# A block product by seven: sums left to accumulating matmuls in a PSUM bank that is read in between

## The chip, the cores and the metric

The kernel runs on one core of a Trainium2 chip. The metric is the time of one execution in microseconds of the device, lower is better. Three runs of the kernel before took 3091.07 to 3096.7 us, with a median of 3095.03 us.

## The reference, cut to what matters

Three transformer layers on one sequence of S = 1024 tokens and D = 1024 features, in fp32. The change lies in the last part alone, the feed-forward network of the third layer:

```python
h  = rmsnorm(x, g_ffn) * (1 + scale2) + shift2                 # [1024, 1024]
up = causal_dwconv(h @ w_up, conv_w, conv_b)                   # w_up [1024, 5632], three taps a column
gate, val = split(up, 2)
x  = x + (1 + gate2) * ((silu(gate) * val) @ w_down)           # w_down [2816, 1024]
out = rmsnorm(x, g_final)
```

## The kernel before

Activations lie transposed: features on the 128 partitions, tokens along a row, in two halves of 512. Each fp32 operand is split into two parts (a rounded one, `hi`, and the rest, `lo`), and a product of operands takes three matmuls a chunk of 128 features (`mm3`): hi by hi, hi by lo, lo by hi. A split costs a cast on ACT (`operand`, L443) and a subtraction (`lo`, L169) on DVE or POOL.

The feed-forward network multiplies by the seven products of Strassen's algorithm in Winograd's form. `strassen` takes two blocks of 128 rows of weights (a pair) and both halves of tokens and of the contraction, and forms products P1 to P7, 12 matmuls of 128x512 each, so 84 for a pair. From them come four quarters of the result: c11 and c12 (tile `u`), c21 and c22 (tile `v`):

```
c11 = P1 + P2          U2 = P1 + P6         U3 = U2 + P7
c12 = U2 + P5 + P3     c22 = U3 + P5        c21 = U3 + P4
```

Before, each product has a PSUM bank of its own. P5 and P7 take the two halves (two banks) of a tile `s` of 1024 columns, of which there are two buffers; the others take tiles `m` of one bank, of which there are four. P1 and P5 are copied to SBUF by ACT (L493, L503). DVE adds c11 (L496), U2 (L505), U3 (L507), and the last terms of c12 (L509) and c21 (L510), each from one operand in PSUM and one in SBUF; POOL adds P5 to U2 and to U3 (L506, L508), all in SBUF.

There are 22 pairs for `w_up`, one block of the gate and one of the value each. A pair is followed by its two convolutions (`conv`: one ACT instruction, L1525, then two on DVE, L1527, for each of the two), the silu (ACT, L1542) and the product of gate and value (POOL, L1543). Then come twice four pairs for `w_down` (16 of the 22 chunks of the contraction; results go to DRAM as `y`), and the last six chunks by plain products (`down`), with the norm and the output.

`start_pairs` begins a group of pairs: for the first three pairs P1 and P2, which need the first token half alone; then the operands of the other products (`turn_ops`, 20 splits); then the rest of these three pairs. These are the early pairs: three for `w_up`, and three for each half of `w_down`, nine in all. The other 21 pairs run P1 to P7 in one go.

Weights' operands lie in tiles `wh`, of which there are eight, and for a cast into one of them ACT waits until PE has used it. A list scheduler sets the order on each engine, from the order of the program's text as priority and its own estimate of times. On the chip each engine works its queue strictly in order and waits for others by semaphores. Such a wait goes by tile: an instruction that writes one half of `s` also waits for earlier readers of its other half.

Of the kernel before, what the change touches and what calls it, by code (L numbers as in the profile page):

```python
# [18 lines left out]
S = 1024  # L19
# [25 lines left out]
def alternate(a, b):  # L45
    """steps of a and of b together"""
    for _ in a:
        next(b, None)
        yield
    yield from b  # L50
# [7 lines left out]
def ahead(tc, gen, offset):  # L58
    """steps of gen, scheduled before work that was emitted up to offset instructions earlier"""
    if not offset:  # L60
        yield from gen
        return
    while True:
        with tc.high_priority(offset):
            x = next(gen, drain)
        if x is drain:
            return
        yield x


def some(g, n):
    """n steps of g"""
    for _ in range(n):
        if next(g, drain) is drain:
            return
        yield


def merge(main, fill, lead=0):
    """emit one step of fill after each step of main"""  # L80
# [7 lines left out]
def pace(main, total, early, fill, n):  # L88
    """steps of early at once, then n steps of fill spread over main, whose steps give their weight"""
# [11 lines left out]
class Net:  # L101
# [18 lines left out]
    def load(self, tag, shape, dt=F32):  # L120
        """a tile to be loaded, but not long before its phase"""
# [10 lines left out]
    def t(self, tag, shape, dt=F32):  # L132
        """a tile of 4 KB a partition, seen in the shape"""
# [14 lines left out]
    def c(self, shape, name, dt=F32):  # L148
        """a constant, or columns that stay"""
# [8 lines left out]
    def small(self, cols, tag):  # L158
        """columns for a short time: the next of a few in turn"""
# [11 lines left out]
    def wblock(self, src, k, m, lo_eng=None):  # L171
        """src: DRAM [k*128, m]; returns [(hi, lo)] per contraction chunk, each [128, m]"""
        return self.wload([src], k, m, lo_eng)

    def wload(self, srcs, k, m, lo_eng=None):
        """blocks of columns side by side"""
# [10 lines left out]
    def mm3(self, out, ws, rs, start=True, stop=True):  # L187
        """out += sum_k ws[k]^T rs[k]; ws, rs: (hi, lo)"""
        n, last = 0, 3 * len(ws) - 1
        for (wh, wl), (rh, rl) in zip(ws, rs):  # L190
            for l, r in ((wh, rh), (wh, rl), (wl, rh)):
                self.nc.tensor.matmul(out, l, r, start=start and n == 0, stop=stop and n == last)  # L192
                n += 1

# [20 lines left out]
    def columns(self, tile_name, width, names):  # L215
        """vectors as columns [128, j]"""
# [23 lines left out]
    def mask_tile(self, name, op, pattern, mult):  # L240
        """0 where the condition holds, else -BIG"""
# [39 lines left out]
    def sigmoid(self, sg, z, src):  # L281
        """sg <- sigmoid(z); src: where |z| is read from (z or its PSUM source)"""
# [15 lines left out]
    def modulation(self, cs, w, bcol, names, acc_tag="t2", w_tag="wr", shared=()):  # L298
        """columns [128, 8] of each 1024 outputs of cs @ w + b; chunks in shared: on ScalarE and GpSimd"""
# [27 lines left out]
    def sum_cols(self, acc, out):  # L327
        """out [128, 8] <- sums over the partitions of acc"""
# [7 lines left out]
    def modulation_first(self, cs, w, bcol, g, nme, acc_tag, w_tag):  # L336
        """as modulation, half of the products on TensorE"""
# [24 lines left out]
    def scale_col(self, g, scale, name):  # L362
        """g * (1 + scale)"""
# [14 lines left out]
    def stat_sum(self, acc):  # L378
        """sum over partitions, on every partition (PSUM)"""
# [10 lines left out]
    def rsqrt_mean(self, out, sums, dim):  # L390
        """(sums / dim + eps)^-1/2"""
# [5 lines left out]
    def stat_end(self, acc, dim):  # L397
        """acc -> (sum over partitions / dim + eps)^-1/2 on every partition, in place"""
        return self.rsqrt_mean(acc, self.stat_sum(acc), dim)

    def new_xt(self, tags):
        """x^T of a token half: 8 chunks [128, 512] in len(tags) tiles"""
# [37 lines left out]
    def operand(self, x, tag="h4", eng=None):  # L440
        """x [128, 512], split"""
# [5 lines left out]
    def rows(self, w, c0, m=128):  # L447
        """loads columns c0.. of w as the rows of a block, by halves of the contraction"""
# [8 lines left out]
    def weights(self, load, early):  # L457
        """operands of two blocks of rows by the number of the product, the first two products' first"""
# [20 lines left out]
    def strassen(self, load, ops, box, tag, early=False):  # L479
        """two blocks of rows times h, [128, 1024] each; early: the products of the first token half, alone,  # L480
        in steps"""
# [4 lines left out]
        def product(ps, i):  # L486
            wv = ws[i].rearrange("p l (k m) -> p l k m", k=4)
            self.mm3(ps, [(wv[:, 0, k], wv[:, 1, k]) for k in range(4)], [(t[:, 0], t[:, 1]) for t in ops[i]])
# [3 lines left out]
        c11, p1 = u[:, 0:512], u[:, 512:]  # L492
        nc.scalar.copy(p1, product(self.pm(), 1))  # L493
        if early:
            yield
        nc.vector.tensor_add(c11, product(self.pm(), 2), p1)  # L496
        if early:
            yield
        next(wg)
        v, t = self.t(tag, [128, S]), self.t("t2", [128, 2, 512])  # L500
        c12, c21, c22, p5, u2 = p1, v[:, 0:512], v[:, 512:], t[:, 0], t[:, 1]
        ps = self.pS()
        nc.scalar.copy(p5, product(ps[:, 0:512], 5))  # L503
        p7 = product(ps[:, 512:], 7)
        nc.vector.tensor_add(u2, product(self.pm(), 6), p1)  # L505
        nc.gpsimd.tensor_add(c12, p5, u2)  # L506
        nc.vector.tensor_add(u2, p7, u2)  # L507
        nc.gpsimd.tensor_add(c22, p5, u2)  # L508
        nc.vector.tensor_add(c12, product(self.pm(), 3), c12)  # L509
        nc.vector.tensor_add(c21, product(self.pm(), 4), u2)  # L510
        box += [u, v]

    def next_h(self, proj, xbox, acc, acol, shift):
        """ends the projection; h of the next part (fp32, in the place of x), and the operands of its first
        token half"""
# [16 lines left out]
    def turn_ops(self, ops, b11, b12, b21, b22):  # L532
        """operands of a chunk of each half of the contraction, but the first two products'; in place"""
# [11 lines left out]
    def start_pairs(self, pair, n, chunk, ops):  # L545
        """the first pairs of blocks: what needs the first token half, the other operands, the rest"""
# [13 lines left out]
    def load_x(self):  # L560
        """tokens of x"""
# [1129 lines left out]
```

## Time and profile before

| what | value |
|---|---|
| time, median of 3 runs | 3095.03 us (3091.07 to 3096.7) |
| span of the profiled execution | 3102.5 us |
| PE busy over the span | 2673.2 us (86%) |
| feed-forward network, from the first early P5 to the end | 2364 to 3102.5 us |
| PE idle in the 362 us of non-early up pairs | 12.4 us |

The page gives the profiled execution its span, from the first to the last instruction, and no other time; that span is 7.5 us (0.24%) longer than the median of the runs. Busy times of PE are modelled from pipelined matmuls, so distances between starts are the surer measure of its pace.

### The profile page before, as it was taken

Reading aid. Unit: us, or ns where it says so; the run is one execution under the profiler, and the core shown is the slowest. Engines: PE = TensorE matmul, PEld = TensorE weight load, DVE = VectorE, ACT = ScalarE, POOL = GpSimd, SP = SyncE. Lnnn points to the kernel's source line nnn. Section 1 sums busy time; section 2 is a strip of 40 time slices with the busy share of each in tenths; the row PEclk is TensorE's granted clock in tenths of the full one; section 3 lists DMA queues with packets and bytes.
Section 4 is the critical chain, followed back from the end, with each engine's and each line's share of the span. In section 5 each row is a group of like instructions: output and inputs, shape, how many; then the busy total and the mean of one; then the engine's idle time right before and its main releaser. Section 6 shows DMA issues by size and latency. Waiting matters only on the chain. (4 is left out here: it accounts for less than half of the span.)

```text
span 3102.5 us, 34630 instructions
## 1 busy us (share of the span) xinstructions
PE 2673.2 (86%) x12023; PEld 2154.1 (69%) x12023; DVE 2110.7 (68%) x2888; ACT 1434.4 (46%) x2609; POOL 1292.2 (42%) x775
## 2 busy tenths in 40 slices
PE   7899999999989957778789689888887999998897
PEld 4677777777767746567667567777675777776776
DVE  7787778766653365555566756377876888889865
ACT  5455554556444423334345444366743444444332
POOL 2323333223353522112124333244545877787761
PEclk8999999999999978889899899999998999998998
DMA  7433333224441352321334235533361222224664
GB/s 268 132 93 96 105 94 90 72 67 118 122 122 53 117 178 78 100 83 53 103 106 131 68 81 82 107 82 100 97 195 46 77 82 75 82 89 149 210 213 153
DMA packets 316225, 338.90 MB, mean 109 GB/s; under 512 B 37060, under 2 KB 239892, under 8 KB 316052
## 3 DMA queue, kind: packets, MB, share of 16 engines
q1 hardware_dynamic: 316052, 336.69, 37.0%
q8 instruction: 96, 1.57, 0.2%
q14 instruction: 77, 0.63, 0.1%
HBM read 231.17 MB, written 60.89 MB: 94 GB/s over the span
## 5 line engine op out<-in xcount | busy, mean ns | idle before, releaser
L192 PE MATMUL m<-h,wh 128*128 128x512 f32 x4744 | 1399.6, 404 | 59.3 <-ACT wh L183 18.6
L192 PEld LDWEIGHTS m<-h,wh 128*128 128x128 f32 x4744 | 912.1, 195 | 269.3 <-ACT wh L183 21.0
L192 PE MATMUL m<-h,wl 128*128 128x512 f32 x1472 | 590.3, 403 | 10.1 <-POOL wl L169 10.0
L169 POOL TENSOR_TENSOR wl<-wr,wh 128x1024 fp32r<-128x1024 f32 (+1 forms) x146 | 329.4, 2263 | 577.6 <-PE m L192 184.4
L761 ACT CAST pt<-m 128x256 fp32r<-128x256 f32 (+1 forms) x632 | 221.2, 369 | 367.8 <-DVE pt L169 192.1
L192 PEld LDWEIGHTS m<-h,wl 128*128 128x128 f32 x1472 | 286.5, 195 | 75.3 <-POOL wl L169 12.5
L169 DVE TENSOR_TENSOR pt<-m,pt 128x256 fp32r<-128x256 f32 (+2 forms) x652 | 256.8, 416 | 103.2 <-ACT pt L761 81.7
L741 ACT ACTIVATE e<-s,cf 128x1024 f32<-128x1024 f32 x192 | 214.8, 1120 | 163.6 <-DVE cf L738 140.2
L737 DVE TENSOR_REDUCE cf<-s 128x1 f32<-128x1024 f32 x192 | 232.6, 1218 | 70.6 <-PE s L682 38.6
L757 PE MATMUL m<-cr,e 128*128 128x128 f32 x1240 | 197.1, 285 | 61.3 <-DVE t L1104 31.4
L757 PEld LDWEIGHTS m<-cr,e 128*128 128x128 f32 x1240 | 155.3, 147 | 89.4 <-issue 53.4
L192 PE MATMUL s<-h,wh 128*128 128x512 f32 x720 | 182.8, 399 | 35.9 <-DVE h L169 17.1
L865 POOL TENSOR_SCALAR e<-e,cf 128x1024 f32<-128x1024 f32 x64 | 82.0, 1281 | 303.8 <-DVE cf L742 286.6
L681 PE MATMUL s<-kk,qq 128*128 128x512 f32 (+3 forms) x376 | 154.0, 415 | 51.6 <-ACT e L741 22.4
L1527 DVE SCALAR_TENSOR_TENSOR e<-z,cf,e 128x1023 f32<-128x1023 f32 (+1 forms) x88 | 175.8, 2008 | 24.8 <-ACT e L1525 24.6
L183 ACT CAST wh<-wr 128x1024 fp32r<-128x1024 f32 (+2 forms) x134 | 122.2, 915 | 145.5 <-PE m L192 67.6
L192 PE MATMUL m<-pt,v 128*128 128x512 f32 x768 | 187.7, 394 | 0.8 <-DVE pt L169 0.6
L192 PEld LDWEIGHTS s<-h,wh 128*128 128x128 f32 x720 | 136.3, 191 | 71.8 <-DVE h L169 18.9
L192 PEld LDWEIGHTS m<-pt,v 128*128 128x128 f32 x768 | 143.9, 189 | 31.6 <-DVE pt L169 1.5
L1099 POOL TENSOR_SCALAR e<-e,cf 128x1024 f32<-128x1024 f32 x64 | 72.8, 1141 | 213.8 <-DVE cf L742 210.0
L682 PE MATMUL s<-kk,qq 128*128 128x512 f32 (+3 forms) x376 | 146.0, 396 | 0.2 <-DMA qq<-pt 0.2
L169 DVE TENSOR_TENSOR wh<-wl,wh 128x512 fp32r<-128x512 f32 x90 | 120.6, 1358 | 19.1 <-ACT wh L443 19.0
(368 smaller groups left out, 4582.3 us busy)
## 6 DMA issues: line engine op xcount, KB each, us to landing
wr<-in_w_out_dram SPq DMA_DIRECT2D x48, 512.0 KB
tb<-in_w_ada_dram SPq DMA_DIRECT2D x48, 512.0 KB
wr<-in_w_up_dram SPq DMA_DIRECT2D x47, 512.0 KB
wr<-in_w_in_dram SPq DMA_DIRECT2D x45, 512.0 KB
qq<-ab SPq DMA_DIRECT2D x144, 128.0 KB
wr<-in_ada_w_dram SPq DMA_DIRECT2D x32, 512.0 KB
tf<-act SPq DMA_DIRECT2D x30, 512.0 KB
wr<-in_w_down_dram SPq DMA_DIRECT2D x30, 512.0 KB
```

Source lines behind the costliest of these rows:

```text
L169: (eng or self.nc.vector).tensor_sub(lo, src, hi.bitcast(F32))
L183: nc.scalar.copy(hi, raw)
L192: self.nc.tensor.matmul(out, l, r, start=start and n == 0, stop=stop and n == last)
L681: nc.tensor.matmul(ps, q(0, j), kk[:, ks], start=True, stop=False)
L682: nc.tensor.matmul(ps, q(1, j), kk[:, ks], start=False, stop=stop)
L737: nc.vector.reduce_max(nm, ps, axis=AX, negate=True)
L741: nc.scalar.activation(e, ps, AF.Exp, bias=nm, scale=scale, accum_out=sm)
L757: nc.tensor.transpose(ps[:, i], p[:, kt * 128:(kt + 1) * 128], self.ident)
L761: nc.scalar.copy(hi, ps[:, i:i + m])
L865: nc.gpsimd.tensor_scalar(e1, e1, r1, self.neglam, ALU.mult, ALU.mult)
L1099: nc.gpsimd.tensor_scalar(e, e, r, 1.0, ALU.mult, ALU.mult)
L1527: nc.vector.scalar_tensor_tensor(t[:, sh:], u[:, 0:S - sh], col(i), t[:, sh:], ALU.mult, ALU.add)
```

## The change

`strassen` now sums in PSUM. A tile `s` of two banks serves a pair: in `sums` P1 is formed, copied out by ACT, and P6 is added to it by matmuls that go on accumulating (U2); that is copied out by ACT, P7 is added (U3), DVE reads it for c22, P4 is added, and ACT copies the result out as c21. In `other` P5 is formed, copied out, and P3 is added; DVE adds U2 to it for c12. P2 alone has a tile `m`. So a pair that is not early has three sums on DVE instead of five, none on POOL instead of two, and four copies on ACT instead of two. In early pairs P1 goes to a tile `m` as before, `sums` holds P6, P7 and P4 without P1, POOL adds P1 to P5 once, and DVE has five sums as before. The order of the products in the text is 1, 2, 5, 6, 3, 7, 4 for the 21 pairs, and 1, 2, 5, 6, 7, 4, 3 for the early ones. Comments are dropped too, so line numbers shift by about 15.

```diff
-    def mm3(self, out, ws, rs, start=True, stop=True):
+    def mm3(self, out, ws, rs, start=True, stop=True, more=False):
...
-                self.nc.tensor.matmul(out, l, r, start=start and n == 0, stop=stop and n == last)
+                self.nc.tensor.matmul(
+                    out, l, r, start=start and n == 0, stop=stop and n == last, skip_group_check=more)
...
-        c11, p1 = u[:, 0:512], u[:, 512:]
-        nc.scalar.copy(p1, product(self.pm(), 1))
+        c11, c12 = u[:, 0:512], u[:, 512:]
+        p1 = c12
         if early:
+            nc.scalar.copy(p1, product(self.pm(), 1))
             yield
-        nc.vector.tensor_add(c11, product(self.pm(), 2), p1)
+            nc.vector.tensor_add(c11, product(self.pm(), 2), p1)
+            yield
+            next(wg)
+            ps = self.pS()
+            sums, other = ps[:, 0:512], ps[:, 512:]
+        else:
+            ps = self.pS()
+            sums, other = ps[:, 0:512], ps[:, 512:]
+            nc.scalar.copy(p1, product(sums, 1))
+            nc.vector.tensor_add(c11, product(self.pm(), 2), p1)
+            next(wg)
+        v, t = self.t(tag, [128, S]), self.t("t2", [128, 2, 512])
+        c21, c22, p5, u2 = v[:, 0:512], v[:, 512:], t[:, 0], t[:, 1]
+        nc.scalar.copy(p5, product(other, 5))
+        product(sums, 6, early)
         if early:
-            yield
-        next(wg)
-        v, t = self.t(tag, [128, S]), self.t("t2", [128, 2, 512])
-        c12, c21, c22, p5, u2 = p1, v[:, 0:512], v[:, 512:], t[:, 0], t[:, 1]
-        ps = self.pS()
-        nc.scalar.copy(p5, product(ps[:, 0:512], 5))
-        p7 = product(ps[:, 512:], 7)
-        nc.vector.tensor_add(u2, product(self.pm(), 6), p1)
-        nc.gpsimd.tensor_add(c12, p5, u2)
-        nc.vector.tensor_add(u2, p7, u2)
-        nc.gpsimd.tensor_add(c22, p5, u2)
-        nc.vector.tensor_add(c12, product(self.pm(), 3), c12)
-        nc.vector.tensor_add(c21, product(self.pm(), 4), u2)
+            nc.vector.tensor_add(u2, sums, p1)
+            product(sums, 7, False)
+            nc.gpsimd.tensor_add(p5, p5, p1)
+            nc.vector.tensor_add(c22, sums, p5)
+            nc.vector.tensor_add(c21, product(sums, 4, False), p1)
+            nc.vector.tensor_add(c12, product(other, 3, False), u2)
+        else:
+            nc.scalar.copy(u2, sums)
+            nc.vector.tensor_add(c12, product(other, 3, False), u2)
+            nc.vector.tensor_add(c22, product(sums, 7, False), p5)
+            nc.scalar.copy(c21, product(sums, 4, False))
```

The order of instructions on every engine is unchanged up to the feed-forward network. Inside it the scheduler weaves pairs into each other. PE's steady order before is P1, P2, P5, P6, P3, P7, P4 of one pair, then the next (ten matmuls of P3 stand ahead of P7, two behind). First PE before, around P7 of one pair. The number after a tile's letter tells buffers apart: `s_18861` holds this pair's P5 and P7, `wh_18845` are P7's weights, `m_18904` is P3's bank and `m_18918` P4's, and h tiles are operands from the tokens:

```order
L192 MATMUL m_18904<-h_3025_18165,wh_18850 128x512
L192 MATMUL s_18861<-h_3012_18116,wh_18845 128x512 [waits Activation_49]
L192 MATMUL s_18861<-h_3012_18116,wh_18845 128x512 x2
L192 MATMUL s_18861<-h_3017_18135,wh_18845 128x512 x3
L192 MATMUL s_18861<-h_3022_18154,wh_18845 128x512 x3
L192 MATMUL s_18861<-h_3027_18173,wh_18845 128x512 x3
L192 MATMUL m_18904<-h_3025_18165,wh_18850 128x512 x2
L192 MATMUL m_18918<-h_3014_18124,wh_18853 128x512 [waits DVE_49]
L192 MATMUL m_18918<-h_3014_18124,wh_18853 128x512 x2
```

P7, the second half of `s_18861`, waits for ACT, the copy of P5 out of the first half. P4 waits for nothing that reads P7.

PE now, the same place in another pair: `s_18784` is this pair's tile, with `wh_18826` the weights of P3, `wh_18821` of P7; `m_19074` is P2 of the pair after the next, `s_18922` with `wh_18955` P5 of the next pair.

```order
L192 MATMUL s_18784<-h_3025_18165,wh_18826 128x512 x3
L192 MATMUL s_18784<-h_3012_18116,wh_18821 128x512 [waits DVE_49]
L192 MATMUL s_18784<-h_3012_18116,wh_18821 128x512 x2
L192 MATMUL s_18784<-h_3017_18135,wh_18821 128x512 x3
L192 MATMUL s_18784<-h_3022_18154,wh_18821 128x512 x3
L192 MATMUL s_18784<-h_3027_18173,wh_18821 128x512 x3
L192 MATMUL m_19074<-h_2943_17667,wh_19056 128x512 [waits Activation_49]
L192 MATMUL m_19074<-h_2943_17667,wh_19056 128x512
L192 MATMUL s_18922<-h_3011_18112,wh_18955 128x512 [waits Activation_49]
L192 MATMUL s_18922<-h_3011_18112,wh_18955 128x512 x2
```

P7 now follows P3 at once, and its first matmul waits for DVE, for the sum c12 that reads what P3 has just finished in the other half of the tile. Behind it two matmuls of a later pair's P2 wait for ACT, for the cast into `wh_19056`. Then comes P5 of the next pair, and only behind that P4 of this pair, which waits for DVE, for c22.

ACT now, from the copy of this pair's U2 (L522) on: `wh_19056` is cast behind a wait for PE (the last matmul of P7 above, whose weights lay in that buffer), and the copy of the next pair's P1 (L507) stands behind it.

```order
L522 COPY t_3123_18836<-s_18784 128x512 [waits PE_49]
L444 CAST wh_18967<-wr_18950 128x512 [waits DMAHW7_49]
L444 CAST wh_18970<-wl_18952 128x512 [waits PE_49]
L444 CAST wh_19053<-wr_19051 128x512 [waits DMAHW1_49,DVE_49,Activation_49]
L1540 ACTIVATE e_18902<-z_18783,cf 128x1024 [waits DVE_49]
L444 CAST wh_19056<-wr_19051 128x512 [waits PE_49]
L507 COPY z_18921<-s_18922 128x512 [waits DMAHW3_49,Pool_49]
```

DVE before, from c12's last term on. `e` tiles are those of the convolutions (`e_18932` of the gate, which reads `z_18807`, the tile of c11 and c12).

```order
L509 TENSOR_TENSOR z_18807<-m_18904,z_18807 128x512 [waits PE_49]
L1527 SCALAR_TENSOR_TENSOR e_18932<-z_18807,cf,e_18932 128x1023 [waits Activation_49]
L510 TENSOR_TENSOR z_18859<-m_18918,t_3140_18860 128x512 [waits PE_49]
L169 TENSOR_TENSOR wh_19089<-wr_19087,wh_19089 128x512 [waits DMAHW7_49,DMAHW1_49,Activation_49]
L1527 SCALAR_TENSOR_TENSOR e_18932<-z_18807,cf,e_18932 128x1022 [waits DVE_49]
L1527 SCALAR_TENSOR_TENSOR e_18936<-z_18859,cf,e_18936 128x1023 [waits Activation_49]
L169 TENSOR_TENSOR wh_19092<-wr_19087,wh_19092 128x512 [waits PE_49,Activation_49]
```

DVE now, from c12 to c22 of one pair. L523 and L524 are the sums c12 and c22, L1542 the convolution's two instructions (L1527 before).

```order
L523 TENSOR_TENSOR z_18783<-s_18784,t_3123_18836 128x512 [waits PE_49,Activation_49]
L169 TENSOR_TENSOR wh_19053<-wr_19051,wh_19053 128x512 [waits DMAHW1_49,Activation_49]
L1542 SCALAR_TENSOR_TENSOR e_18902<-z_18783,cf,e_18902 128x1023 [waits Activation_49]
L1542 SCALAR_TENSOR_TENSOR e_18902<-z_18783,cf,e_18902 128x1022 [waits DVE_49]
L524 TENSOR_TENSOR z_18835<-s_18784,t_3123_18836 128x512 [waits DMAHW7_49,PE_49,Pool_49]
L169 TENSOR_TENSOR wh_19056<-wr_19051,wh_19056 128x512 [waits Activation_49]
```

Before, the last read of PSUM (L510) stands behind one instruction of a convolution, and nothing on PE waits for it at once. Now c22, for which P4 waits, stands behind both instructions of the gate's convolution, and these wait for ACT's part of it, which waits for c12.

In the stretches of early pairs PE before weaved P5 of two pairs with P6, P3 and P4 of the first, chunk by chunk, while their operands were made: 60 matmuls. Now only P5 of two pairs, 24 matmuls, is woven there, and P6 to P3 come behind. At the end the last pair's P6, P3, P7 and P4 now stand between the products of `down`.

## Rows read from the trace of the kernel before

**Rows 1.** The page: span, and PE's busy time, share of the span and instructions.
```profile
span 3102.5 us, 34630 instructions
...
PE 2673.2 (86%) x12023; PEld 2154.1 (69%) x12023; DVE 2110.7 (68%) x2888; ACT 1434.4 (46%) x2609; POOL 1292.2 (42%) x775
```

**Rows 2.** Busy time by stretch (us): PE, PEld, DVE, ACT, POOL; granted clock, DMA share, GB/s.
```profile
2364.00:2446.00 82.00, 63.67 (x242) 47.78 (x242) 69.45 (x63) 35.57 (x54) 63.96 (x38) 0.90 0.15 45
2446.00:2808.00 362.00, 349.58 (x1511) 283.28 (x1511) 316.47 (x259) 154.73 (x224) 289.63 (x165) 1.00 0.28 87
2808.00:2868.00 60.00, 44.85 (x165) 34.10 (x166) 57.02 (x49) 23.97 (x41) 49.50 (x28) 0.83 0.45 145
2868.00:2928.00 60.00, 60.00 (x263) 49.17 (x263) 46.57 (x52) 24.01 (x44) 44.66 (x30) 1.00 0.71 233
2928.00:2956.00 28.00, 17.84 (x62) 13.55 (x62) 25.59 (x22) 10.88 (x21) 22.35 (x14) 0.82 0.32 103
2956.00:3005.00 49.00, 47.73 (x210) 38.86 (x209) 36.01 (x33) 18.97 (x27) 38.92 (x23) 1.00 0.69 235
3005.00:3102.50 97.50, 75.30 (x353) 61.83 (x351) 51.36 (x71) 23.61 (x62) 15.92 (x7) 0.91 0.48 168
```

**Rows 3.** Timeline of ACT: the gate's silu in two pairs that lie 12 apart.
```profile
2502.22 1.06 ACT L1542 ACTIVATE e<-e 128x1024 f32<-128x1024 f32 x1 [0.60 <-DVE e L1527]
...
2743.07 1.06 ACT L1542 ACTIVATE e<-e 128x1024 f32<-128x1024 f32 x1 [0.60 <-DVE e L1527]
```

**Rows 4.** Timeline of PE in the steady stretch: start, length, instruction, [idle before <-releaser].
```profile
2609.02 8.78 PE L192 MATMUL m<-h,wh 128*128 128x512 f32 x38
2617.63 2.88 PE L192 MATMUL s<-h,wh 128*128 128x512 f32 x12
2621.54 4.83 PE L192 MATMUL m<-h,wh 128*128 128x512 f32 x20 [0.57 <-POOL wh L169]
2626.20 2.88 PE L192 MATMUL s<-h,wh 128*128 128x512 f32 x12
```

**Rows 5.** Groups by line and shape, 2446 to 2808 us: count | busy, mean ns | idle before <-releasers.
```profile
L192 PE MATMUL m<-h,wh 128*128 128x512 f32 x1079 | 254.1, 391 | 7.1 <-POOL wh L169 7.1
L192 PE MATMUL s<-h,wh 128*128 128x512 f32 x432 | 106.1, 395 | 8.8 <-ACT t L503 8.8
...
L1527 DVE SCALAR_TENSOR_TENSOR e<-z,cf,e 128x1023 f32<-128x1023 f32 x37 | 78.5, 2122 | 24.6 <-ACT e L1525 24.6
...
L1527 DVE SCALAR_TENSOR_TENSOR e<-z,cf,e 128x1022 f32<-128x1022 f32 x37 | 67.2, 1816 | 0.1
...
L1525 ACT ACTIVATE e<-z,cf 128x1024 f32<-128x1024 f32 x36 | 44.8, 1245 | 104.5 <-DVE z L509 50.0 <-POOL wh L169 34.9 <-POOL z L508 17.1
...
L505 DVE TENSOR_TENSOR t<-m,z 128x512 f32<-128x512 f32 x18 | 12.2, 678 | 0.0
```

**Rows 6.** Timelines of ACT and PE: a cast behind PE, a product behind a copy.
```profile
2629.12 0.62 ACT L443 CAST wh<-wr 128x512 fp32r<-128x512 f32 x1 [0.17 <-PE s L192]
...
2394.02 0.58 ACT L503 COPY t<-s 128x512 f32<-128x512 f32 x1
...
2394.65 3.02 PE L192 MATMUL s<-h,wh 128*128 128x512 f32 x12 [0.29 <-ACT t L503]
```

**Rows 7.** Timelines of DVE and POOL where one's work meets the other's.
```profile
2616.33 2.32 DVE L1527 SCALAR_TENSOR_TENSOR e<-z,cf,e 128x1023 f32<-128x1023 f32 x1 [1.31 <-ACT e L1525]
...
2616.28 1.29 POOL L169 TENSOR_TENSOR wh<-wr,wh 128x512 fp32r<-128x512 f32 x1
2617.52 2.27 POOL L508 TENSOR_TENSOR z<-t 128x512 f32<-128x512 f32 x1
```

**Rows 8.** Timeline of PE behind the first three pairs.
```profile
2429.20 3.71 PE L192 MATMUL m<-h,wh 128*128 128x512 f32 x10 [2.52 <-DVE wh L169]
...
2446.02 4.36 PE L192 MATMUL s<-h,wh 128*128 128x512 f32 x12 [3.63 <-ACT t L503]
```

**Rows 9.** Waits of PE from 3005 us on: us in total, times, longest.
```profile
PE m L192 <- DVE wl L169: 3.5, 2, 2.0
```

More of the change, by code (lines that the diff above doesn't have):

```diff
@@ L484, in strassen, with product @@
         ws = next(wg)
-        def product(ps, i):
+        def product(ps, i, start=True):
             wv = ws[i].rearrange("p l (k m) -> p l k m", k=4)
-            self.mm3(ps, [(wv[:, 0, k], wv[:, 1, k]) for k in range(4)], [(t[:, 0], t[:, 1]) for t in ops[i]])
+            wk = [(wv[:, 0, k], wv[:, 1, k]) for k in range(4)]
+            self.mm3(ps, wk, [(t[:, 0], t[:, 1]) for t in ops[i]], start, more=True)
             return ps
         u = self.t(tag, [128, S])
-        c11, p1 = u[:, 0:512], u[:, 512:]
```

## Prediction

> **What bounds the kernel now.** I read the page first, for the whole: the span is 3102.5 us and PE is busy in 86% of it [rows 1]. The change touches the feed-forward network alone, so next come the busy times by stretch from 2364 us on [rows 2]. The reader is to see three kinds of stretch. From 2446 to 2808 us, where the non-early up pairs run, PE is busy 349.6 of 362 us at a granted clock of 1.00: it is PE's stretch, though DVE (316 us) and POOL (290 us) are near. In the two short stretches in which operands for `w_down` are made (2808 to 2868 and 2928 to 2956) DVE is busy 57 of 60 and 25.6 of 28 us, and PE is idle for 15 and 10 us; the same happens from 2364 us, mixed with the first pairs. The last 97.5 us have 22 us without PE.
>
> Then the period of the steady stretch. The silu of the gate stands once in each pair; two of them, 12 pairs apart, start at 2502.22 and 2743.07 us [rows 3], so a pair takes 240.85 / 12 = 20.07 us. PE's own part: 38 matmuls start from 2609.02 to 2617.63 us [rows 4], so one takes 8.61 / 38 = 0.2267 us and the 84 of a pair 19.04 us. A pair thus loses 1.03 us. The groups say to whom [rows 5]: matmuls into `m` waited 7.1 us for POOL's split of P6's weights, those into `s` 8.8 us for ACT's copy of P5, in 18 pairs together (1511 matmuls / 84). In rows 4 the first of these is the 0.57 us before 2621.54. PE waits for nothing of DVE here: results wait in four `m` banks until DVE comes to them.
>
> **The change, part by part, in a steady pair.** Removed: two POOL sums and two DVE sums; added, two ACT copies (ACT is busy 155 of 362 us [rows 2], and has room). The vector work that goes is not what PE waits for, except through POOL's queue; if both old waits vanish entirely, the pair falls to 19.04 us, 1.03 less. That is the most that can be gained there.
>
> Added are waits of PE on what reads the bank. I take them in the order now on PE, with P3's end as zero, and handoffs from rows: a cast behind PE starts at 2629.12 us [rows 6], while the 12 matmuls that it waits for began at 2626.20 [rows 4] and had their slots until 2626.20 + 12 x 0.2267 = 2628.92; so PE to a reader 0.20 us. A reader to PE: the copy of P5 ends at 2394.60, the product waiting behind it starts at 2394.65: 0.05 us [rows 6]. That same row shows that the wait on the other half of a tile is real time, since this product writes another bank than the copy reads.
>
> - P7 stands right behind P3 and waits for c12. A DVE sum from PSUM takes 0.68 us [rows 5]. The gap: 0.20 + 0.68 + 0.05 = 0.93 us. DVE is free for it, as the convolution ahead of it (of the pair before) is over some 5 us earlier in this walk.
> - Two matmuls of P2 stand right behind P7 and wait for a cast into the buffer that P7's weights leave. Cast 0.62 us [rows 6]: 0.20 + 0.62 + 0.05 = 0.87 us.
> - P5 of the next pair waits for the copy of P1, which ACT does behind that cast. Cover is the two P2 matmuls, 0.45 us; a copy takes 0.58 us [rows 6] and starts about 0.1 us before the cast's end: 0.05 us.
> - P4 waits for c22. It could start at 0.93 + 2.72 (P7) + 0.87 + 0.45 + 0.05 + 2.72 (P5) = 7.74 us. On DVE c12 ends at 0.88; ACT's part of the convolution, 1.25 us, at 2.15; DVE's two parts, 2.12 and 1.82 us on average [rows 5], at 6.15; c22 at 6.85. No wait, with 0.9 us to spare. Had both parts the long form, 2.3 us each, it would be 7.5: still none. Were the two gaps above not there, P4 could start at 5.89, and would wait 1.0 to 1.6 us: so this chain holds the pair to 20.0 us even then.
> - P3 waits for the copy of U2, P6 for that of P5, P1 for that of c21. Between each and its wait stand 12 to 24 matmuls (2.7 to 5.4 us), against 0.2 + 0.58 + 0.05 us; I cost these at nothing. The price without cover is 0.8 us each.
>
> Sum: 19.04 + 0.93 + 0.87 + 0.05 = 20.89 us, against 20.07: 0.82 us more a pair, and with 18 pairs **+15 us**. Bounds: 20.0 (no gap, only the chain of c22) to 22 (c22 later by one more POOL instruction of 1.1 us), so -1 to +35 us.
>
> A rule of the Trainium skill speaks for the lower end. The page "PSUM — Partial Sum Buffer", section "PSUM bank collisions raise a hardware error", asks to guard PSUM by bank and quadrant and to read another bank while matmuls run. By it P7 need not wait for c12, which lies in the other bank; a pair would take 20.0 to 20.7 us. Rows 6 show the tile-wide wait kept, so I sum with it.
>
> **The starts.** While operands are made, PE now does 24 matmuls in place of 60. What counts is its idle time until the next dense stretch. First start: 30 matmuls more remain when the operands are there, 6.8 us; but before, PE then lost 2.52 + 3.63 us behind the first convolutions [rows 8], and walking the new order with P3, P5 and P4 of the early pairs behind c21, c12 and c22 I find stalls of about 1, 1 and 2 to 4 us there. Together +2 us (-3 to +8). Second start: PE now waits in each pair until DVE has done c22, so DVE trails it by less, and the operands are ready sooner after the last up pair, by 5 to 10 us (an estimate from the walk above: what DVE still has behind c22 there is about one pair's two convolution parts and splits less); against it 23 to 30 more matmuls (5 to 7 us) remain, some at half clock: 0 (-6 to +8). Third start: the idle 10 us [rows 2] were the wait for operands, and it remains; P7 and P4 of the pair before stand between: 0 (-3 to +8). The six early pairs and two others of `w_down` have about three handoffs of 0.9 us without cover: +2.5 us (0 to 5).
>
> **The end.** P6, P3, P7 and P4 of the last pair fill places where PE waited 3.5 us for split weights [rows 9], but its stores and loads come later: -2 us (-3.5 to +3).
>
> Total: 15 + 2 + 0 + 0 + 2.5 - 2 = +17.5 us. The profiled span of 3102.5 us becomes 3120; the median of the runs is 7.5 us shorter, so **3112.5 us**. I take 3113.
>
> **Rivals.** First, faster: DVE and POOL hold each other up, and the change relieves both. A convolution's part begun at 2616.33 ends at 2618.65, after a POOL instruction (2616.28 to 2617.57) and 1.1 us more; the POOL instruction begun at 2617.52 in turn lasts 2.27 us [rows 7]. A sum with one operand in PSUM always takes 0.68 [rows 5]. Each POOL sum removed takes up to 1.1 us off a DVE instruction, 2.2 us a pair. The mechanism: if c12 and the cast come early enough that P7 and P2 do not wait, and the convolution's two parts, 1.1 us shorter each, let c22 end at 4.7, before P4 at 5.89, a pair takes 19.1 us: -18 us there, and 3077 in all. It decides where P7's wait is under 0.1 us. Against it, P7's wait begins with the end of P3 itself, so no relief of DVE can make it shorter than 0.9 us. Chance 0.07. The Trainium skill states this as a rule ("SBUF — State Buffer", section "Who interferes with whom"): a DVE instruction with two SBUF inputs contends with a GpSimd instruction that reads SBUF, one with at most one does not. By that rule, which rows 7 and 5 agree with, what goes on POOL is worth more than its own time.
>
> Second, no change: c12's wait costs 0.4 less than I say, or P4's takes the place of the others, and a pair stays near 20.1 us; the starts give 0 to +4. Then 3091 to 3101. For it: the chain of c22 alone gives 20.0. Against: the two handoffs are on PE itself. Chance 0.07.
>
> Third, much slower: c22 falls behind a further POOL instruction or the cast behind a waiting ACT instruction, a pair takes 21.9 us (+33), and the starts lose 10 more at half clock, as from 2808 us, where the granted clock was 0.83 [rows 2]. Then 3145. For it: DVE is busy 87% of the stretch. Against: the change takes 1.4 us a pair from it. Chance 0.09.
>
> **The numbers.** My forecast, slower by 7 to 40 us, has a chance of 0.77. A difference of 0.2% (6 us) is about the least that a measurement of this kernel can tell from none. The range leaves out the first rival and the far end of the third: 3098 to 3135 us. Faster by over 0.2%: 0.07; within: 0.07; slower: 0.86.
>
> **What would show it.** Right: in the steady stretch matmuls into `s` wait for DVE's c12 (L523) 0.9 us in each pair, and those into `m` for ACT's cast (L444) 0.9 us; waits for POOL's splits gone; silus 20.9 us apart; c22 done before PE asks for it; DVE and POOL busy less. Wrong in the sum: PE waiting for L524 too, or another period. Wrong in the starts: more than 5 us of new idle at one of them. The prediction fails as a whole if these waits are there but shorter than 0.5 us each, or if the starts gain over 10 us from DVE being ahead.

## The result, and the profile after

The changed kernel takes 3147.99 us (median of 4 runs, 3144.15 to 3150.47) against 3093.2 us (median of 4): a ratio of 1.0177, 95% interval 1.0162 to 1.0191, so 55 us slower. The sign was foretold. The time lies outside the range of 3098 to 3135 us, and the loss of 55 us is three times the 17.5 us forecast.

The page of the changed kernel, to be held against [rows 1]:

```profile
span 3142.4 us, 34556 instructions
...
PE 2683.7 (85%) x12023; PEld 2153.4 (69%) x12023; DVE 1984.7 (63%) x2846; ACT 1465.1 (47%) x2651; POOL 1193.9 (38%) x724
```

PE has the same 12023 matmuls; DVE is busy 126 us less and POOL 98 us less, and the kernel is slower. The work that the change removes was not what PE waited for.

The two spans differ by 40 us, the medians by 55. A span of the trace is 1.75 us less than the time of its run here (3142.4 and 3144.15 us), so the profiled execution of before, at 3102.5, was itself some 11 us slower than the median of its kernel's runs. Most of that lies ahead of the feed-forward network, which the change does not touch: over all profiles here, the first early P5 starts between 2349.85 and 2366.43 us. So I compare from the first early P5 on. It starts at 2364.44 us before and at 2349.85 us after; from there to the end it is 738.1 us before and 792.6 after, 54.5 us more, which is the whole difference of the medians.

**Where it goes.** The program's order says which matmul stands behind each start in the trace, so two products can be used as milestones: the time lost between them is the time that passes less 0.2267 us for each matmul of P1 to P7 started in between. The first milestone is P7 of the eighth up pair. Before and after, first early P5 and that P7, in PE's timeline:

```profile
2364.44 0.73 PE L192 MATMUL s<-h,wh 128*128 128x512 f32 x2 [1.73 <-ACT h L443]
...
2526.90 1.43 PE L192 MATMUL s<-h,wh 128*128 128x512 f32 x5 [0.88 <-ACT t L503]
```

```profile
2349.85 0.73 PE L192 MATMUL s<-h,wh 128*128 128x512 f32 x2 [1.72 <-ACT h L444]
...
2539.61 1.66 PE L192 MATMUL s<-h,wh 128*128 128x512 f32 x6 [0.85 <-DVE z L523]
```

Before, 162.46 us pass for 574 matmuls, 32.3 us lost; after, 189.76 us for 600 (products of the next pair come earlier), 53.7 us lost. In the same way for all stretches and, in advance, for the experiments (us lost; the last column is the difference of the sums):

| kernel | first start, to P7 of pair 8 | steady, 12 pairs | second start, to the second half of `w_down` | third start, to P5 of its last pair | end, with what is not P1 to P7 | against before |
|---|---|---|---|---|---|---|
| before | 32.3 | 12.3 | 24.7 | 14.3 | 99.4 | |
| changed | 53.7 | 23.6 | 41.6 | 16.0 | 102.6 | +54.5 |
| late pairs only | 37.5 | 21.7 | 31.4 | 13.7 | 96.0 | +17.2 |
| early pairs only | 43.9 | 12.3 | 34.6 | 20.9 | 101.2 | +29.9 |
| changed, one-bank tiles | 29.1 | 0.0 | 28.8 | 10.7 | 93.9 | -20.6 |
| late only, one-bank tiles | 28.7 | 0.0 | 19.2 | 11.0 | 95.9 | -28.3 |
| changed, tiles split for early pairs | 37.5 | 23.6 | 35.4 | 20.5 | 99.9 | +33.8 |
| changed, tiles split for late pairs | 40.8 | 0.0 | 33.8 | 17.9 | 100.8 | +10.3 |
| copy of P5 behind P6 | 46.8 | 23.3 | 44.2 | 17.3 | 97.9 | +46.3 |
| one-bank tiles, order of the changed | 50.5 | 8.5 | 41.6 | 15.4 | 97.2 | +30.1 |
| before, one-bank tiles | 22.9 | 10.8 | 21.1 | 18.0 | 96.0 | -14.3 |
| early of before and late of changed, one-bank tiles | 29.1 | 0.0 | 19.1 | 10.6 | 106.9 | -17.5 |

These are single executions, and the ratios of many runs below decide; the table tells the place.

**The steady stretch costs nearly what was forecast.** Two silus of the gate, 12 pairs apart [rows 3]:

```profile
2502.86 1.07 ACT L1557 ACTIVATE e<-e 128x1024 f32<-128x1024 f32 x1 [1.04 <-DVE e L1542]
...
2755.04 1.06 ACT L1557 ACTIVATE e<-e 128x1024 f32<-128x1024 f32 x1 [1.57 <-DVE e L1542]
```

252.18 / 12 = 21.015 us a pair, 0.94 more than the 20.07 of before; the forecast was 20.89. PE's timeline there, and PE's waits between those silus (line waited for: us in total, times, longest):

```profile
2602.78 3.02 PE L192 MATMUL s<-h,wh 128*128 128x512 f32 x12 [0.85 <-DVE z L523]
2605.63 0.61 PE L192 MATMUL m<-h,wh 128*128 128x512 f32 x2
2606.47 5.75 PE L192 MATMUL s<-h,wh 128*128 128x512 f32 x24 [0.22 <-ACT z L507]
...
2614.33 8.32 PE L192 MATMUL s<-h,wh 128*128 128x512 f32 x36
2623.50 3.01 PE L192 MATMUL s<-h,wh 128*128 128x512 f32 x12 [0.85 <-DVE z L523]
2627.22 0.73 PE L192 MATMUL m<-h,wh 128*128 128x512 f32 x2 [0.71 <-ACT wh L444]
```

```profile
PE s L192 <- DVE z L523: 10.2, 12, 0.9
PE m L192 <- ACT wh L444: 4.2, 6, 0.7
PE s L192 <- ACT z L507: 1.3, 6, 0.2
```

P7 waits for c12 in each of the 12 pairs, P2 for the cast in every second one, and in the others P5 for the copy of P1. No wait for L524 (c22), none for POOL's splits.

**The starts cost far more.** PE's timeline in the first start; its waits there, from 2350 to 2435 us; and its waits for operands (`h`) before, from 2364 to 2446 us:

```profile
2383.80 8.59 PE L192 MATMUL s<-h,wh 128*128 128x512 f32 x36 [0.81 <-ACT t L512]
2396.95 5.39 PE L192 MATMUL s<-h,wh 128*128 128x512 f32 x12 [4.56 <-DVE z L518]
2403.12 5.74 PE L192 MATMUL s<-h,wh 128*128 128x512 f32 x24 [0.78 <-DVE z L519]
2411.56 7.38 PE L192 MATMUL s<-h,wh 128*128 128x512 f32 x24 [2.71 <-DVE z L518]
```

```profile
PE s L192 <- ACT h L444: 9.7, 4, 2.7
PE s L192 <- DVE h L169: 8.8, 2, 6.0
PE s L192 <- DVE z L518: 7.3, 2, 4.6
```

```profile
PE s L192 <- DVE h L169: 6.0, 1, 6.0
PE m L192 <- DVE h L169: 3.2, 5, 0.8
...
PE m L192 <- ACT h L443: 2.1, 2, 1.2
PE s L192 <- ACT h L443: 1.7, 1, 1.7
```

Three things add up. PE waits longer for operands, 18.5 us against 13.0, as it has only the two P5 to do. It then waits for c22 (L518), behind which P4 stands in the same bank. And its clock is lower. The first 82 us of the stretch by engine, for the row that begins 2364.00 in [rows 2]:

```profile
2350.00:2432.00 82.00, 56.29 (x191) 41.06 (x192) 50.51 (x53) 29.15 (x44) 46.07 (x31) 0.75 0.10 32
```

191 matmuls in place of 242, and a granted clock of 0.75 in place of 0.90: in this stretch PE paused more, and was granted the lower of its two levels (1.2 and 2.4 GHz) for a larger part of the time. The 12 matmuls of P4 behind the wait of 4.56 us took 5.39 us, 0.45 each, about twice the 0.2267 of the steady stretch. Of the 21.4 us that the first start loses more, waits make 14.7 (35.3 us from the first P5 to P7 of pair 8, against 20.6); the other 6.7 are matmuls that start further apart.

The longest of these waits is not what the walk of the prediction had looked for. DVE, then POOL:

```profile
2396.20 0.69 DVE L518 TENSOR_TENSOR z<-s,t 128x512 f32<-128x512 f32 x1 [5.09 <-POOL wh L169]
```

```profile
2392.35 1.26 POOL L469 TENSOR_TENSOR wl<-wr 128x512 f32<-128x512 f32 x1 [3.72 <-DMA wr<-in_w_up_dram]
...
2394.91 1.26 POOL L169 TENSOR_TENSOR wh<-wr,wh 128x512 fp32r<-128x512 f32 x1
```

The first pair's P7 is over by 2389.24 us (24 matmuls after 2383.80) and its P5 + P1 as well, yet the sum starts 0.03 us after POOL's split of weights of the third pair, which had waited for their load. None of its operands comes from there. The program's waits name exactly this split, the last reader of those raw weights, and the built program puts the sum's output at the same address in SBUF as them. So this wait is for a buffer, not for data; a kernel with another buffer there was not tried.

At the end, the last wait of PE before the final norm, 5.82 us before, is 10.81 us. PE before, then PE and DVE now:

```profile
3051.34 1.19 PE L192 MATMUL m<-pt,wh 128*128 128x512 f32 x2 [5.82 <-DVE z L1646]
```

```profile
3091.41 1.19 PE L192 MATMUL m<-pt,wh 128*128 128x512 f32 x2 [10.81 <-DVE z L1661]
```

```profile
3089.20 0.75 DVE L1621 SCALAR_TENSOR_TENSOR kk<-e,cf,kk 128x512 f32<-128x512 f32 x1 [3.24 <-DMA kk<-xs]
3089.86 1.40 DVE L1661 SCALAR_TENSOR_TENSOR z<-s,cf,tb 128x512 f32<-128x512 f32 x2
```

The instruction that PE waits for (L1661) stands on DVE behind one that waits 3.24 us for a load of `xs`.

### The profile page after: what moved, and what is told of

Its sections match the earlier page's. It is cut to its first block, busy times and chain, and to the rows that moved or that the text cites. A ratio compares the mean times of both kernels' runs of the same rounds, so it can differ in the third digit from the quotient of the medians.

```text
span 3142.4 us, 34556 instructions
## 1 busy us (share of the span) xinstructions
PE 2683.7 (85%) x12023; PEld 2153.4 (69%) x12023; DVE 1984.7 (63%) x2846; ACT 1465.1 (47%) x2651; POOL 1193.9 (38%) x724
## 5 line engine op out<-in xcount | busy, mean ns | idle before, releaser
L192 PE MATMUL m<-h,wh 128*128 128x512 f32 x3412 | 1077.0, 405 | 47.2 <-ACT wh L183 17.7
L192 PEld LDWEIGHTS m<-h,wh 128*128 128x128 f32 x3412 | 654.6, 195 | 195.1 <-ACT wh L183 19.5
L192 PE MATMUL s<-h,wh 128*128 128x512 f32 x2052 | 517.9, 408 | 81.6 <-ACT h L444 17.6
L192 PEld LDWEIGHTS s<-h,wh 128*128 128x128 f32 x2052 | 397.1, 197 | 193.7 <-DVE z L523 21.6
L772 PEld LDWEIGHTS m<-cr,e 128*128 128x128 f32 x1240 | 155.7, 147 | 90.1 <-issue 53.7
L1542 DVE SCALAR_TENSOR_TENSOR e<-z,cf,e 128x1023 f32<-128x1023 f32 x88 | 137.4, 1561 | 26.4 <-ACT e L1540 25.6
L696 PEld LDWEIGHTS s<-kk,qq 128*128 128x128 f32 x376 | 75.9, 202 | 71.7 <-ACT e L756 29.2
```

The lines of the kernel that those rows point to most:

```text
L696: nc.tensor.matmul(ps, q(0, j), kk[:, ks], start=True, stop=False)
L772: nc.tensor.transpose(ps[:, i], p[:, kt * 128:(kt + 1) * 128], self.ident)
L1542: nc.vector.scalar_tensor_tensor(t[:, sh:], u[:, 0:S - sh], col(i), t[:, sh:], ALU.mult, ALU.add)
```

## The experiments

Ratios are against the kernel before on the same chip, with their 95% interval; "us" is the ratio less 1, times 3100.

**1, 2. One part of the pairs at a time.** For run 1, the early branch has the seven products and sums of before, as here, and the other branch stays as changed; for run 2 it is the other way round.

```diff
         if early:
...
-            product(sums, 7, False)
-            nc.gpsimd.tensor_add(p5, p5, p1)
-            nc.vector.tensor_add(c22, sums, p5)
-            nc.vector.tensor_add(c21, product(sums, 4, False), p1)
-            nc.vector.tensor_add(c12, product(other, 3, False), u2)
+            nc.gpsimd.tensor_add(c12, p5, u2)
+            nc.vector.tensor_add(u2, p7, u2)
+            nc.gpsimd.tensor_add(c22, p5, u2)
+            nc.vector.tensor_add(c12, product(self.pm(), 3), c12)
+            nc.vector.tensor_add(c21, product(self.pm(), 4), u2)
```

> Only the 21 pairs that are not early use the new sums; the nine early pairs have the sums of before, with banks of their own. Theory A (the 37 us beyond the steady stretch are lost by the early pairs, whose P6, P7 and P4 follow each other in one bank with a DVE sum between each two): the steady period stays at 21.0 us, each start returns to what it was before to within 4 us, and the whole is 3093 + 17 = 3110 us, at most 3116. Theory B (the late pairs' last products run into the next start and wait there for DVE): the second start keeps 15 us or more of the loss, and the whole is 3130 us or more.

> Only the nine early pairs use the new sums, the 21 others those of before. Theory A: the steady period is 20.07 us again, the starts keep their loss of some 35 us, whole 3124 to 3132 us. Theory B: starts lose at most 12 us, whole 3093 to 3106 us.

Run 1: 1.0059 (1.0043 to 1.0075), +18 us. Run 2: 1.0088 (1.0072 to 1.0103), +27 us. The numbers set for them were reckoned from 3093 us, and the kernel before took 3099.15 beside these runs, so I go by the ratios. Theory A stands for run 1 (+17 us set, +23 at most); run 2 is some 4 us below theory A's +31 to +39 and far from theory B's 0 to +13. The late pairs cost the forecast sum, the early pairs alone more than that. Theory B is not empty: in run 1 the second start loses 6.7 us more than before, 4.8 without its two steady pairs. Together the parts give 46 us of the 55. The steady waits of run 1 are those of the changed kernel, from 2510 to 2738 us (L524 is c12 there, L516 the copy of P1):

```profile
PE s L192 <- DVE z L524: 9.4, 11, 0.9
PE m L192 <- ACT wh L444: 2.8, 4, 0.7
PE s L192 <- ACT z L516: 1.6, 7, 0.2
```

**3, 4. A tile for each bank.** The same sums in two banks, declared as two tiles of 128x512 (there are two buffers of either), so that a matmul waits for readers of its own bank alone:

```diff
-        ps = self.pS()
-        sums, other = ps[:, 0:512], ps[:, 512:]
+        sums, other = self.pT('a'), self.pT('b')
```

> The whole change, but the two banks of a pair are two tiles of one bank each, so that no instruction waits for a reader of the other bank. The order on PE changes with it. If the wait by tile is what P7 pays (0.85 us in a pair), the matmuls of P7 no longer wait for c12; the chain of c22 then sets the pair to about 20.0 us (an estimate from the durations in the profile of before), 1.0 less than 21.0, so 3148 - 18 = 3130 us. If PE only waits elsewhere for the same DVE work, the period stays at 21.0 us and the whole within 5 us of 3148.

> Late pairs alone with the new sums, in two tiles of one bank. If both theories hold (early pairs cost 35 us, the wait by tile 1 us a pair), it is 3093 to 3098 us, level with the kernel before; with a period of 19.2 us, which needs c22 ready before P4, 3080 us.

Run 3: 0.9927 (0.9912 to 0.9942), -23 us. Run 4, late pairs alone: 0.9919 (0.9903 to 0.9935), -25 us. Run 3 was expected at 3130 us and took 3078.86: the declaration of one tile as two is worth 77 us (1.0177 less 0.9927), far more than either theory had. Run 4 is 5 us below the lowest number set for it. In the steady stretch of either PE is never idle, 228 of 228 us at clock 1.00. Run 3:

```profile
2510.00:2738.00 228.00, 228.00 (x1007) 188.81 (x1006) 150.91 (x145) 113.17 (x168) 156.04 (x85) 1.00 0.26 83
```

The scheduler chose another order as well: in every second steady pair ten matmuls of a later P1 stand between P3 and P7, P3 stands before P7 in the first two early pairs, and nine matmuls of P6 are again woven with P5 while operands are made. So the runs don't yet say whether the waits or the order cost the time.

**5, 9. The waits alone.** As run 3, but every matmul of P1 to P7 is held in the order of the changed kernel (`seq`) by an edge that sets the order of issue and waits for nothing:

```diff
+        for a, b in zip(seq, seq[1:]):
+            self.tc.add_manual_dep(b, a.name, how, reason="pin")
```

> The two tiles of one bank of the split run, with every matmul of the seven products on PE held in the order of the changed kernel; so the tiles alone differ. Theory A (the waits by tile themselves cost the time): P7 no longer waits in the steady stretch, the period falls from 21.0 to about 20.0 us (the chain of c22 then holds P4), the first start loses less by 5 to 10 us, whole 3115 to 3125 us. Theory B (the waits cost little by themselves, the order that the scheduler had to choose around them does): less than 10 us of the 75 between the changed kernel and the split run come back, 3138 us or more. Theory C (all of it is the waits): within 5 us of the split run, 3079 us.

> As the pinned run, but exact: in the run before, the P5 of two early pairs, which the changed kernel forms chunk by chunk side by side, went one behind the other; here PE's order of all matmuls is that of the changed kernel, and only the shared tile is two tiles. Theory A (in the starts the order costs: P6 cannot begin before the copy of P5, so PE has 24 matmuls in place of 60 while operands are made, and the rest comes later): the starts keep 10 us or more each, the steady period is 19.76 us as in the run before, whole 3115 to 3126 us. Theory B (the waits by tile cost in the starts as well): the first start comes back to within 5 us of the kernel before, whole 3100 us or less.

Run 5: 1.0080 (1.0063 to 1.0096). Run 9, with the exact order: 1.0096 (1.0079 to 1.0113), +30 us. By the ratios both lie within theory A's numbers (+22 to +32 and +22 to +33 us over 3093). One clause of it fell in run 5, where the first start was to lose 5 to 10 us less: it loses 50.9 us, 2.9 less. The steady stretch loses 8.5 us where the changed kernel loses 23.6; what is left there from 2541 to 2781 us is the cast alone:

```profile
PE m L219 <- ACT wh L473: 5.1, 8, 0.7
```

The first two starts keep 18.1 and 16.9 us of loss over before (the third 1.1, where the changed kernel has 1.7), though no wait by tile in PSUM is left. Run 9's first 82 us, and PE's waits in them:

```profile
2363.30:2445.30 82.00, 55.46 (x188) 41.02 (x189) 51.32 (x55) 29.88 (x45) 46.09 (x31) 0.75 0.11 32
```

```profile
PE b L219 <- ACT h L473: 9.8, 4, 2.7
PE b L219 <- DVE h L196: 8.8, 2, 6.1
PE a L219 <- DVE z L539: 8.6, 3, 4.7
```

The row is that of the changed kernel again. PE's waits in run 3, from 2361 to 2443 us:

```profile
PE b L197 <- DVE h L174: 7.9, 2, 6.0
PE a L197 <- DVE h L174: 2.9, 3, 2.0
PE b L197 <- ACT h L449: 1.7, 1, 1.7
PE a L197 <- ACT z L520: 1.6, 1, 1.6
...
PE a L197 <- ACT h L449: 0.6, 2, 0.3
```

In the order of run 9, PE waits 18.6 us for operands and 8.6 us for c22 (L539), which reads the bank that P4 goes on in; in that of run 3, 13.1 us for operands and not at all for c22. So of the 77 us between the changed kernel and run 3 about 25 are waits by tile (1.0177 less 1.0096), nearly all in the steady pairs, and about 52 lie in the order that the scheduler takes where it need not keep the two banks together. That order also covers most of the waits that accumulating itself brings; in the order of the changed kernel they stay open.

**6, 7. Split tiles for one part of the pairs.**

The line of run 3 stands in the early branch alone (run 6) or in the other alone (run 7):

```diff
-            ps = self.pS()
-            sums, other = ps[:, 0:512], ps[:, 512:]
+            sums, other = self.pT('a'), self.pT('b')
```

> Early pairs with a tile for each bank, late pairs with the shared tile of two. If the loss of early pairs is only the shared tile's, they cost nothing once it is split: level with the run that changes late pairs alone, 3118 us, to within 6 us. If it is the accumulating in one bank (P6, then P7, then P4, with a DVE sum read between), the loss of 28 us stays: 3140 us or more.

> Early pairs with the shared tile, late pairs with a tile for each bank. If costs add: late pairs in two tiles gave -24 us, early pairs in the shared tile +28 us, so about +4 us, 3103 us, with a steady period of 19.04 us. If early and late pairs cost more together than apart, as the changed kernel's 55 us against 18.5 + 28.4 hints, 3110 us or more.

Run 6: 1.0099 (1.0081 to 1.0117), +31 us. That is neither of its two numbers. The first start is that of run 1 to the tenth, 37.5 us: there, once the tile is split, accumulating in one bank costs no more than the sums of before. The second and third start lose 4.0 and 6.8 us more than in run 1, the end 3.9; so some 12 us of the early pairs' 27 remain, and why they do so in the down pairs alone is open. Run 7: 1.0016 (1.0002 to 1.0031), +5 us, as the sum foretold, and the steady stretch loses nothing: the early pairs' loss does not depend on that of the late ones here.

**8. The copy of P5 behind P6, in early pairs.**

```diff
-nc.scalar.copy(p5, product(other, 5))
-product(sums, 6)
+product(other, 5)
+product(sums, 6)
+nc.scalar.copy(p5, other)
```

> The shared tile everywhere; in early pairs the copy of P5 stands behind the matmuls of P6 in the program, so that P6 no longer waits for a reader of the other bank and may be formed chunk by chunk beside P5. The readers' handoffs (u2, c22, c21) stay. If the early pairs lose by the wait of P6 for the copy of P5 and by the lack of work while operands are made, the starts regain 10 us or more, 3138 us or less. If they lose by the chain P6, u2, P7, c22, P4, it stays within 5 us of 3148 us.

1.0143 (1.0121 to 1.0165). The median of 3146.06 us looks like the second case, but the kernel before took 3100.16 us beside it, and by the ratio it is 10 us less than the changed kernel, as the first case had it. The two intervals overlap a little, so the size is not firm. The first start gains 6.9 us, the second loses 2.6 more. Freeing P6 from the copy may help, but the scheduler still formed both P5 almost wholly before P6, so the run tells little of the lack of work.

**10, 11. Is it the sums at all?** Run 10 is the kernel before with its own sums, P5 and P7 in a tile of one bank each; run 11 is that for early pairs with the late pairs of run 4:

```diff
-        ps = self.pS()
-        nc.scalar.copy(p5, product(ps[:, 0:512], 5))
-        p7 = product(ps[:, 512:], 7)
+        nc.scalar.copy(p5, product(self.pT('a'), 5))
+        p7 = product(self.pT('b'), 7)
```

> The kernel before with its own sums, but P5 and P7 in a tile of one bank each. If the shared tile alone made the difference, the steady wait for ACT's copy of P5 (8.8 us in 18 pairs) goes and the one for POOL's weights (7.1 us) stays: 3100 - 9 = 3091 us. If the late pairs' gain in the split runs comes from summing in PSUM (less work on DVE and POOL), this kernel stays within 5 us of 3100, and 15 us or more above the split runs.

> Early pairs with the sums of before, late pairs with the new sums, all products in tiles of one bank. Late pairs alone in two tiles gave 24 us; if the early pairs gain by P7 no longer waiting for the copy of P5, 2 to 6 us more: 3070 us. If their order suffers from it, 3076 us or more.

Run 10: 0.9939 (0.9923 to 0.9956), -19 us, with none of the change. Both its cases fall: it gains twice the 9 us, and stands 4 and 6 us above runs 3 and 4, not 15. POOL's splits went too, as the order is another. In the steady stretch one single wait is left, from 2510 to 2738 us:

```profile
PE m L197 <- ACT wh L449: 8.3, 1, 8.3
```

and that one comes from vector work. ACT, then DVE, then POOL of run 10:

```profile
2654.72 0.62 ACT L449 CAST wh<-wl 128x512 fp32r<-128x512 f32 x1 [5.05 <-DVE wh L174]
```

```profile
2648.81 5.88 DVE L174 TENSOR_TENSOR wh<-wl,wh 128x512 fp32r<-128x512 f32 x3
2654.61 0.68 DVE L525 TENSOR_TENSOR t<-m,z 128x512 f32<-128x512 f32 x1
```

```profile
2648.46 2.34 POOL L1563 TENSOR_TENSOR e<-e,e 128x1024 f32<-128x1024 f32 x1 [4.24 <-DVE e L1547]
2650.88 1.59 POOL L474 TENSOR_TENSOR wl<-wr 128x512 f32<-128x512 f32 x1
2652.55 1.59 POOL L478 TENSOR_TENSOR wl<-wl,wr 128x512 f32<-128x512 f32 x1
```

Three splits take 5.88 us, 1.96 each, while POOL works without a pause, and the cast starts behind them. None of the instructions on POOL here is a sum that the change removes, so it is not shown that the new sums would save this wait. Run 11: 0.9946 (0.993 to 0.9962), -17 us, its second case: its first four stretches are those of run 4, its end 11 us longer. Run 4 is the fastest; its interval overlaps those of runs 3, 10 and 11, so no gain of the new sums over the split tile alone is shown.

## Why the prediction was right and wrong

**What bounds the kernel: right.** PE sets the steady pair; DVE at 144 of 252 us in the changed kernel, far less busy than the 316 of 362 in [rows 2], gave nothing.

**The steady sum: right, with errors in its terms that cancel.** The terms were reckoned from the end of PE's slots, so they are to be held against starts, not against the idle time of the rows. P7 behind c12 was put at 0.93 us. The 36 matmuls from 2614.33 have their slots until 2622.49, and P7 starts at 2623.50: 1.01. The 12 matmuls behind the wait then take 2.85 us to the next start (2602.78 to 2605.63) where 12 x 0.2267 = 2.72 would do, so 1.14 in all. The cast was put at 0.87 in each pair; it is 0.87 by starts (2623.50 + 2.85 to 2627.22), but in every second pair only. In the others the copy of P1, put at 0.05, takes 0.39 (2605.63 + 0.45 to 2606.47). c22 is done before P4 asks, as the walk said. In 18 pairs 0.94 makes +17 us, against +15: the slow matmuls behind each wait, which had no term, and the longer copy make up for the casts that are not there.

**The bound from c22: wrong.** The prediction held that this chain keeps the pair at 20.0 us even without the two gaps. In run 9, without P7's gap, a pair takes 19.04 + 8.5 / 12 = 19.75 us and PE waits for the cast alone; in run 3 it takes 19.04. The chain was reckoned with convolution parts of 2.12 and 1.82 us [rows 5]. Grouped by shape between the two silus, the changed kernel has them at 1.46 and 1.73, with POOL busy 158 of 252 us where it was 290 of 362; that this is the reason was not tried alone:

```profile
L1542 DVE SCALAR_TENSOR_TENSOR e<-z,cf,e 128x1022 f32<-128x1022 f32 x24 | 41.5, 1728 | 0.4
L1542 DVE SCALAR_TENSOR_TENSOR e<-z,cf,e 128x1023 f32<-128x1023 f32 x24 | 34.9, 1456 | 12.8 <-ACT e L1540 12.8
```

**The starts: this step failed.** "Together +2 us (-3 to +8)" for the first, 0 for the second and the third, and +2.5 for handoffs of early pairs. Measured, without the steady pairs in those stretches at 0.94 each: 53.7 - 32.3 - 4 x 0.94 = +17.6, then 41.6 - 24.7 - 2 x 0.94 = +15.0, and +1.7; together 34 us where 4.5 were put. The prediction's own sign for this, over 5 us of new idle at a start, came true. For the first start the walk had the lack of work right (24 matmuls where there were 60), but set it against the two waits of 2.52 and 3.63 us [rows 8] as if these would go for nothing, took 4 to 6 us of stalls where the three on DVE and the one on ACT above make 8.9, and left out the clock. Run 9 shows that the loss follows the order: with the same order and no wait by tile it stays. Runs 3 and 6 show that accumulating alone does not cost it: with split tiles and an order of the scheduler's own, the first start loses about as much in run 3 as before (29.1 against 32.3, where the steady pairs in it make the difference), and as much in run 6 as in run 1. The order in turn is the tile's, as its declaration is all in which run 3 differs from the changed kernel. The step between is argued, not shown: P6 lies in the tile of which the copy of P5 reads the other half, so it is not woven with P5; but run 8, which moves that copy, has almost the same order there. The prediction named that wait for the product behind the copy of P5 [rows 6], but did not carry it on to the starts, where PE lacks the work that covered the making of operands.

**The end: wrong by 5.2 us.** -2 was put for the splits that PE waited for [rows 9]. They are gone, but the last wait of PE became 5 us longer; the stretch lost 3.2 us. That loads come later was the prediction's reservation, and the trace shows one of them (3.24 us on DVE) ahead of what PE waits for.

**The rivals.** The first, faster, did not come about: P7 waits 0.85 us. With one-bank tiles its condition (a wait of P7 under 0.1 us) holds, and the gain of 23 and 25 us is near its 18. But the relief of DVE is not needed for that: run 10 has the old sums, DVE busy 206 of 228 us, and stands within 6 us. The second, no change, took c12's wait for 0.4 us shorter, which it is not. The third, much slower, came nearest to the time of the changed kernel (3145), and by luck: its pair of 21.9 us did not come about, the loss in the starts was larger than it said, and its terms (+33 and +10 us with the rest of the sum) make 3140.

**Small slips in the sums.** 8.61 / 38 is 0.2266, which is 0.01 us a pair. By the 60 and 24 of the order 36 matmuls remain in the first start, 8.2 us, where 30 and 6.8 stand. "Slower by 7 to 40 us" and a range from 3098 us (+3) do not agree at the lower end. None of them bears on the outcome.

**The rule on PSUM.** "PSUM — Partial Sum Buffer", section "PSUM bank collisions raise a hardware error", in the Trainium skill asks for guards by bank and quadrant. The prediction weighed it and rightly summed with the wait by tile, which the kernel keeps. Runs 3, 4 and 10 read one bank while matmuls write the other, without a wait between them (PE busy 228 of 228 us in runs 3 and 4), and agree with the rule; its worth was put at 0.2 to 0.9 us a pair, and is 21.015 - 19.04 = 1.97 us, with the order that comes with it.

## What to carry to other kernels

A wait that the program keeps by tile costs twice: the wait itself, here 25 of 77 us, and the order that a scheduler takes to live with it, here the rest. So before sums are moved into a bank that is read in between, see which buffers share a tile with it, and split these first: that alone gave -19 us here without the change. Price a change at the starts and ends of a stretch by the matmuls that still cover a wait, and give the clock a term of its own there: here the granted clock fell from 0.90 to 0.75.

## What the runs showed of the hardware that was not expected

After each wait in the steady stretch PE's next product took 0.13 us more than its matmuls' pace (2.85 against 2.72 us for 12), and the row's idle of 0.85 is 1.01 by starts, so such a wait cost 1.14. In the first start the granted clock fell from 0.90 to 0.75 with the same products spread over more pauses. DVE's split, 0.68 us at 2646.41 us in run 10 where POOL was idle, took 1.96 us on average where POOL worked beside it; each of the three ends 0.55 us after a POOL instruction does. The Trainium skill's "SBUF — State Buffer", section "Who interferes with whom", gives as the reason one shared port pair held by one of the two at a time, and the rows of run 10 agree.
